# Staging buffers, VectorE instead of GpSimd, and a shorter planner lag in a hybrid decoder step on eight cores

## The chip, the cores and the metric

The kernel runs on the 8 cores of one Trainium2 chip, as two dies of four cores (cores 0 to 3 and 4 to 7). Every core does the same work on its own share of the batch, and no data passes between them. A core has TensorE for matmuls (it writes to PSUM, eight banks in this kernel), VectorE, ScalarE and GpSimd for everything else, and DMA engines, 16 by the profile's pages, that move data between DRAM and the on-chip memory SBUF; in this kernel GpSimd also issues the DMAs that load and cast weights. The metric is device time in microseconds (us) of the slowest core. The experiments ran in four sets on four chips, each set beside runs of the kernel before on the same chip. Some executions here are longer at a lower granted TensorE clock: one of the kernel before took 1599.7 us with cores 0 to 3 at 0.82 to 0.83 and the other four at 0.97, where the median beside it was 1439.01 us.

## The reference, cut to what matters

One decoder layer for a prompt group (one sequence of 2048 rows per core) and a sample group (16 sequences of 4 rows per core) with the same weights:

```python
h = x + W_out( sig(gA) * Wa(GLA(xn)) + sig(gB) * Wb(Pool(xn)) )   # xn = rmsnorm(x)
h = h + CrossAttn(rmsnorm(h), K_mem, V_mem)       # 4 heads, 256 memory tokens
h = h + W_down(relu(W_up rmsnorm(h))**2)
# one projection xn @ w_in gives q, k, v, forget gate, og, u, gA, gB
# GLA output: rmsnorm(o) * silu(og);  Pool: windows 2/4/8/16, mixed, then Wb
```

K_mem and V_mem of the prompt are outputs (`mk`, `mv`). So are the GLA states (`sgp`, `sgs`) and the last pooling rows (`spp`, `sps`).

## The kernel before

The prompt's 2048 rows go through in four tiles of 512 rows. The program first records operations, and a planner then orders them for each engine on a simple cost model. The recorder's helpers own the lines of a profile: L789 is every matmul group of one bank, L801 a group of several, L846 every ScalarE activation, L898 every DMA. So profiles of this kernel are read by tile names.

Each operation carries a priority. Work on the side, that is the one-time precomputation of tile 0 (`pre`) and the sample group's matmuls ("hooks", which use a weight while it is loaded), is recorded with an offset of 120 places. The planner then takes it about that much later than its place in the program says. I call this offset the lag:

```python
    def hook(self, name, *a):              # cut
        self.g.pri_off = po + 120
        self.aux = 1
        f(*a)
    def step(self, name, n=1):             # one piece of a generator: pre, G, K, V, P
        self.g.pri_off = po + 120
        self.aux = 1
        ...  next(g)
    def bank(self):                        # PSUM: 5 banks for the tile, 3 for side work
        lo, n = (5, 3) if self.aux else (0, 5)
```

Weights pass through five slots `wt` of 1 MiB; four more slots, `wx`, lie inside `WqK` and `VWo` and serve until those are written. A weight is cast from fp32 at its first two uses by a GpSimd DMA, stored as bf16 to scratch DRAM at the second (at the first for the up and down weights), and read from there afterwards:

```python
    def W(self, name):                     # cut
        elif times == 0 or (times == 1 and name not in EARLY):
            cast, store = True, times == 1 or name in EARLY
        if cast:  self.dma("pool", flat, src, nb=5.0, ahead=60.0, ...)
        else:     self.dma("sp", flat, self.scr[idx], ...)
        if store: self.dma("sp", self.scr[idx], flat, nb=2.5, ...)
```

A slot can be loaded again only when its matmuls and its store are over. Loads stand in GpSimd's instruction stream in order.

The parts that the change touches, cut: the norm's power, the GLA chunk, the output gate, the branch gates, and in the precomputation the pooled weight b' and `mk`, `mv`:

```python
    def rstd(self, st, P, n=1):
        self.ts("dve", st[:P, :n], st[:P, :n], EPS, ALU.add)
        self.tt("pool", st[:P, :n], st[:P, :n], self.ncols[:P, 8:8 + n], ALU.pow)   # ncols: -0.5
    # tile(): og0, og1 and u0 side by side over the four chunks, then u1
            self.tt("pool", Sb, self.S, pv, ALU.mult)          # decayed state as bf16
            self.act(t, pb, AF.Tanh, scale=0.5)                # og; sig = (1 + tanh)/2
            self.stt("dve", ogb, t, 1.0, pb, ALU.add, ALU.mult)
    # branch gates: ug = W("gb0"), uw = W("bp0"): tanh(pb1), then (t + 1) * pb2 -> t1
    # precompute(): pm @ w_b -> bpt (SBUF); then
            self.dma("sp", self.scr[b], self.bpt[n]); ...      # read back as "bp0", "bp1"
            t = self.tb()                                      # one of four shared tmp
            self.cp("act", t, pb); self.dma("sp", O["mk"], t)
            self.cp("pool", self.Mtm, t)
    # sample: t = self.tb(); cp("act", t, pb); 16 x dma("sp", O["sps"][bb, 11:15], t)
```

## Time and profile before

| | before |
|---|---|
| median of 3 runs | 1434.41 us (1433.49 to 1434.5) |
| best of the 15 runs beside the changed kernel, same chip | 1430.65 us |
| span of core 6 in the profile, granted clock | 1432.6 us, 0.969 |
| TensorE / VectorE / ScalarE / GpSimd busy | 92 / 45 / 36 / 12% |

A busy share of 92% on TensorE with everything else under half says that TensorE sets the time and that the interest lies in its holes. The prediction shows where they are. What it calls cold clock is this: in the 6.4 us after the gap of 14.56 us the granted clock was 0.55 (the last 24 of 32 matmuls of 256 columns took 4.76 us, 0.20 each, where they step by 0.11 in solid stretches), in the 3.6 us after the gap of 6.92 us it was 0.50, and after one of 2.82 us 1.00.

```profile
146.03 0.53 POOL L898 DMA_DIRECT2D wt<-wu  x1 [21.62 <-PE pb L801]
...
161.76 0.53 POOL L898 DMA_DIRECT2D wt<-wu  x1 [15.21 <-PE pb L789]
...
175.57 0.53 POOL L898 DMA_DIRECT2D wt<-wu  x1 [13.29 <-PE pb L789]
```

TensorE is full from 160 to 180 us, so no list of TensorE's gaps shows anything here. But the DMA engines are 60% idle, in a stretch where their share is 0.93 in the 20 us before and 1.01 in the 20 us after. GpSimd asked for only three weights in 30 us, because each load stood 13 to 22 us until matmuls ahead of it were done. The first of them, by the built program the precomputation's weight `xo0`, waits for the last matmuls of `xqT0`, the `KT,wt` group at 143.61 us that the prediction shows: side work of the precomputation, which the lag puts late.

### The profile page before, as it was taken

How to read it: one execution, taken by the hardware profiler on the slowest of the kernel's cores; microseconds unless marked ns; L12 is line 12 of the kernel's file. 1: busy time of each engine (PE TensorE's matmuls, PEld its weight loads, DVE VectorE, ACT ScalarE, POOL GpSimd, SP SyncE). 2: the span in 40 equal slices, each digit the busy share in tenths (PEclk: the TensorE clock that was granted, in tenths of full speed). 3: DMA queues.
4: the chain of work that ended last, by engine and by line, in shares of the span. 5: the costliest groups of instructions: out<-in, count | busy, mean ns of one | idle time of the engine just before them, and what ended most of it. 6: DMA issues, size and time to landing. Idle time of an engine off the chain costs nothing.

```text
span 1432.6 us, 21898 instructions; the slowest of 8 cores (1419.1 to 1432.6 us)
## 1 busy us (share of the span) xinstructions
PE 1311.7 (92%) x7843; PEld 653.7 (46%) x7976; DVE 641.5 (45%) x1114; ACT 512.1 (36%) x1012; POOL 176.4 (12%) x232
## 2 busy tenths in 40 slices
PE   6995979999897979999999899989999999999996
PEld 3452434544343434454444455454454454455443
DVE  3652314643553412454586722464344542354344
ACT  3451214721162411662224631562114451372112
POOL 5121011200111200100010300120011230020000
PEclk7998899999998889999999999999999999999998
DMA  9999698989999998734668333358669895621332
GB/s 205 170 178 193 125 205 161 275 172 219 222 218 241 226 243 201 261 135 148 235 238 276 132 119 118 148 131 228 180 175 214 228 229 192 180 87 59 118 118 96
DMA packets 47094, 261.42 MB, mean 182 GB/s; under 512 B 6054, under 2 KB 6510, under 8 KB 23292
## 3 DMA queue, kind: packets, MB, share of 16 engines
q0 software_dynamic: 15584, 85.38, 36.0%
q1 hardware_dynamic: 31404, 174.63, 34.8%
q8 instruction: 66, 1.08, 0.3%
q14 instruction: 40, 0.33, 0.1%
HBM read 287.63 MB, written 56.36 MB: 240 GB/s over the span
## 4 chain that ended last, share of the span: by engine, by line
PE 68%; DMA 21%; ACT 3%; DVE 3%; issue 3%; POOL 1%; SPq 0%; DVEq 0%; ACTq 0%; POOLq 0%
PE pb L789 62%; DMA wt<-wu 9%; DMA sps<-tmp 3%; PE pb L801 3%; DMA wscratch<-wt 3%; DMA wx<-wscratch 2%; ACT tmp L846 2%; PE pb L822 2%; PE pb L812 2%; DMA mv<-tmp 2%; DMA wt<-wscratch 1%; DMA xh<-xp 1%; DVE stat L884 0%; ACT xn L846 0%; DVE actT L858 0%
## 5 line engine op out<-in xcount | busy, mean ns | idle before, releaser
L789 PE MATMUL pb<-actT,wt 128*128 128x512 bf16 (+2 forms) x1879 | 402.9, 367 | 15.9 <-DMA wt<-wu 4.5
L846 ACT ACTIVATE tmp<-pb 128x512 f32<-128x512 f32 (+1 forms) x250 | 143.6, 587 | 509.1 <-PE pb L789 371.6
L789 PEld LDWEIGHTS pb<-actT,wt 128*128 128x128 bf16 x1920 | 181.2, 98 | 218.9 <-issue 24.4
L789 PE MATMUL pb<-wt,hid 128*128 128x512 bf16 x994 | 227.1, 381 | 8.3 <-DMA wt<-wu 5.4
L789 PE MATMUL pb<-wt,actT 128*128 128x512 bf16 x679 | 162.3, 388 | 10.7 <-DMA wt<-wu 4.3
L789 PEld LDWEIGHTS pb<-wt,hid 128*128 128x128 bf16 x1024 | 97.9, 98 | 126.0 <-issue 15.1
L869 DVE SCALAR_TENSOR_TENSOR xh<-pb,r,xh 128x512 f32<-128x512 f32 x128 | 95.8, 751 | 100.7 <-PE pb L789 100.5
L869 DVE SCALAR_TENSOR_TENSOR hid<-pb,tmp 128x512 bf16<-128x512 f32 x128 | 86.6, 689 | 107.0 <-ACT tmp L846 107.0
L858 POOL TENSOR_TENSOR stat<-stat,ncols 128x1 f32<-128x1 f32 (+3 forms) x71 | 47.4, 669 | 515.4 <-DVE stat L864 513.0
L789 PEld LDWEIGHTS pb<-wt,actT 128*128 128x128 bf16 x704 | 66.7, 99 | 89.3 <-issue 21.9
L846 ACT ACTIVATE xn<-xh 128x512 bf16<-128x512 f32 (+1 forms) x81 | 56.4, 704 | 125.5 <-DVE xh L869 111.1
L898 POOL DMA_DIRECT2D wt<-wu x57 | 31.5, 554 | 405.1 <-PE pb L789 291.7
L789 PE MATMUL pb<-o2T,wt 128*128 128x512 bf16 x251 | 61.1, 387 | 10.2 <-ACT tmp L846 10.0
L869 DVE SCALAR_TENSOR_TENSOR t<-tmp,pb 128x512 f32<-128x512 f32 x32 | 22.0, 687 | 106.2 <-PE pb L789 60.4
L789 PE MATMUL pb<-WqK,actT 128*128 128x512 bf16 x249 | 57.7, 379 | 2.0 <-ACT tmp L846 0.9
L789 PE MATMUL pb<-VWo,PT 128*128 128x512 bf16 x247 | 56.9, 379 | 2.1 <-ACT tmp L846 1.7
L789 PE MATMUL pb<-dT,wt 128*128 128x512 bf16 x223 | 53.3, 383 | 5.9 <-ACT tmp L846 3.4
L789 PE MATMUL pb<-wt,mT 128*128 128x512 bf16 x248 | 56.1, 379 | 2.1 <-DMA wt<-wscratch 1.0
L869 DVE SCALAR_TENSOR_TENSOR tmp<-tmp,pb 128x512 f32<-128x512 f32 (+1 forms) x34 | 22.8, 671 | 63.2 <-PE pb L789 57.5
L822 PE MATMUL pb<-ident,xn 128*128 128x128 bf16 x512 | 40.5, 225 | 9.8 <-DVE xn L864 6.1
L864 DVE TENSOR_SCALAR stat<-stat 128x1 f32<-128x1 f32 (+4 forms) x102 | 20.6, 203 | 58.8 <-ACT xn L846 32.4
L846 ACT ACTIVATE tmp<-pb,stat 128x256 f32<-128x256 f32 (+1 forms) x68 | 37.8, 556 | 23.1 <-DVE stat L884 9.1
(218 smaller groups left out, 1422.7 us busy)
## 6 DMA issues: line engine op xcount, KB each, us to landing
wt<-wscratch SPq DMA_DIRECT2D x87, 1024.0 KB, 5.9
wt<-wu POOLq DMA_DIRECT2D x57, 1024.0 KB, 20.1
wscratch<-wt SPq DMA_DIRECT2D x32, 1024.0 KB, 33.3
land<-xp SPq DMA_DIRECT2D x16, 512.0 KB, 10.3
xh<-xp SPq DMA_DIRECT2D x16, 512.0 KB, 22.0
yp<-xh SPq DMA_DIRECT2D x15, 512.0 KB
s0f<-sgla SPq DMA_DIRECT2D x15, 512.0 KB, 8.3
sgs<-s0f SPq DMA_DIRECT2D x15, 512.0 KB
```

Of the source, the lines that this page charges most:

```text
L789: ins = e.matmul(out, l, r, start=(start and i == 0), stop=(stop and i == m - 1))
L801: ins = e.matmul(out, l, r, start=(i == 0), stop=(i == m - 1))
L812: ins = e.matmul(out, l, r, start=False, stop=last and k == len(al) - 1)
L822: ins = e.transpose(o, i, d)
L846: return self.g.op("act", lambda e: e.activation(out=out, in_=in_, func=func, scale=scale, **kw), reads=rd, writes=wr, cost=c, tab=tab)
L858: return self.g.op(eng, lambda e: e.tensor_tensor(out=out, in0=in0, in1=in1, op=op), reads=[in0, in1], writes=[out], cost=self.vcost(eng, ...
L864: return self.g.op(eng, lambda e: e.tensor_scalar(out=out, in0=in0, scalar1=s1, scalar2=s2, op0=op0, **kw), reads=rd, writes=[out], cost=s ...
L869: return self.g.op(eng, lambda e: e.scalar_tensor_tensor(out=out, in0=in0, scalar=scalar, in1=in1, op0=op0, op1=op1), reads=rd, writes=[ou ...
L898: return self.g.op(q, lambda e: e.dma_start(out=out, in_=in_), reads=[in_], writes=[out], cost=0.6 if q == "pool" else 0.07, dma=True, nb= ...
```

## The change

Its intent is to keep the in-order engines from standing behind one another's waits: ScalarE behind output stores, GpSimd's weight loads behind its arithmetic, weights behind slots that two or three of them hold side by side. Cut to its core (recorder plumbing, sample gates, renamings, and the moves of the softmax product `Pn`, of `pmT` and of the memsets from GpSimd to VectorE left out):

```diff
 # staging buffers; one more tmp
-        self.tmp = [... for i in range(4)]
+        self.tmp = [... for i in range(5)]
+        self.mstage = [g.sb(f"mstage{i}", XH + 8192 + 2048 * i, [128, 512], F32) for i in range(4)]
+        self.ustage = [g.sb(f"ustage{i}", X + o, [64, 512], F32) for i, o in enumerate((7168, 4096))]
-                    t = self.tb()
+                    t = self.ring("mstage", self.mstage)
-                    self.cp("pool", self.Mtm[wh]..., t[:, :])
+                    self.cp("dve", self.Mtm[wh]..., t[:, :])
 # GpSimd keeps only DMA issue; tanh becomes exp, ln, exp
-        self.tt("pool", st, st, self.ncols[:P, 8:8 + n], ALU.pow)
+        self.act(st, st, AF.Ln, bias=EPS);  self.act(st, st, AF.Exp, scale=-0.5)
-                self.tt("pool", Sb, self.S, pv, ALU.mult)
+                self.tt("dve", Sb, self.S, pv, ALU.mult)
-            self.act(t, pb, AF.Tanh, scale=0.5)
+            self.act(t, pb, AF.Exp, scale=-1.0); self.act(t, t, AF.Ln, bias=1.0); self.act(t, t, AF.Exp, scale=-1.0)
 # gates stored at the third use
+STORE_AT.update(dict.fromkeys(("ga0", "ga1", "gb0", "gb1"), 2))
 # b' out of SBUF in tile 0, stored after the attention
-            uw = self.W(f"bp{n}")
+            u = Fixed(self.bpt[n]) if first and br == "b" else self.W(f"{nm}{n}")
 # og0, og1, u0, u1 and the down weights one after another
-        og = [self.W("og0"), self.W("og1")];  u0 = self.W("u0")
+        u = self.W("og0")
+        for s in range(4): ogp(u, 0, s)
+        u = self.W("og1");  ...  u = self.W("u0");  ...  u = self.W("u1")
 # the planner: eight banks placed freely; priorities inherited; the lag
+        for o in reversed(ops):
+            for j in o.succ:
+                o.pri = min(o.pri, ops[j].pri)
     def hook(self, name, *a):
-            self.g.pri_off = po + 120
+            self.g.pri_off = po + 16
     def step(self, name, n=1):
-        self.g.pri_off = po + 120
+        self.g.pri_off = po + (20 if name == "pre" else 120)
```

## The prediction

> **What bounds the kernel now.** I read the table of cores first (spans 1419.1 to 1432.6 us, clocks 0.969 to 0.977, both dies alike: a fast run), then the slices of the page for core 6, the slowest.
>
> ```profile
> PE   6995979999897979999999899989999999999996
> ...
> PEclk7998899999998889999999999999999999999998
> DMA  9999698989999998734668333358669895621332
> ```
>
> Each digit is a slice of 36 us. TensorE is the engine that sets the time (92% busy), but its holes lie in slices 0 to 15, just where the DMA engines are full. From slice 16 on it is nearly solid. So the question is the first 560 us. The forget-gate matmul opens each of the four 512-row tiles, which gives a table of windows by tile:
>
> ```profile
> core 6: us, PE busy (x) PEld busy (x) DVE busy (x) ACT busy (x) POOL busy (x), PEclk, DMA share, GB/s
> 30.50:401.20 370.70, 324.95 (x1746) 160.10 (x1778) 158.75 (x258) 130.01 (x256) 52.94 (x75) 0.96 0.95 193
> 401.20:754.00 352.80, 325.47 (x1781) 154.93 (x1812) 164.62 (x301) 130.76 (x252) 33.53 (x40) 0.96 0.77 215
> 754.00:1091.00 337.00, 321.90 (x2024) 162.92 (x2058) 159.74 (x290) 123.35 (x248) 37.76 (x46) 0.99 0.58 168
> 1091.00:1420.40 329.40, 321.08 (x2139) 163.86 (x2172) 146.69 (x246) 117.99 (x242) 35.21 (x43) 1.00 0.52 154
> ```
>
> What is a tile worth without holes and at full clock? In solid stretches 49 or 50 matmuls of 512 columns take 10.74 us (one record in fifty is missing), 0.215 us each; 256 columns step by 0.11, 128 by 0.056. Counting the built program's matmuls by tile gives 314, 310, 321 and 331 us (estimates; the last is 2 us too high, as that tile took 329). The slack is thus 57, 43, 16 and about 0 us, 116 us in all; before and behind lie 30 us of start (14 of it TensorE work) and 12 us of tail.
>
> Next I listed TensorE's idle stretches and looked at what the engine named there was itself waiting for:
>
> ```profile
> 142.29 0.60 ACT L846 ACTIVATE tmp<-pb 128x512 f32<-128x512 f32 x1 [14.50 <-DMA mk<-tmp]
> ...
> 143.61 1.86 PE L801 MATMUL pb<-KT,wt 128*128 128x256 bf16 x8 [14.56 <-ACT WqK L846]
> ```
> ```profile
> 450.96 0.53 POOL L898 DMA_DIRECT2D wt<-wu  x1 [27.76 <-DMA wscratch<-wt]
> ...
> 458.62 0.37 PE L801 MATMUL pb<-vt,att 128*128 128x256 bf16 x1 [4.75 <-POOL Sb L858]
> ...
> 461.25 1.04 POOL L858 TENSOR_TENSOR stat<-stat,ncols 128x4 f32<-128x4 f32 x1
> ...
> 463.43 0.58 PE L801 MATMUL pb<-vt,kdt 128*128 128x256 bf16 x2 [3.80 <-DVE xn L869]
> ```
> ```profile
> 522.40 1.89 PE L789 MATMUL pb<-o2T,wt 128*128 128x512 bf16 x8 [2.82 <-ACT tmp L846]
> 532.93 3.57 PE L789 MATMUL pb<-o2T,wt 128*128 128x512 bf16 x8 [6.92 <-ACT tmp L846]
> ```
>
> These are two kinds of head-of-line blocking. ScalarE works in order; its next tanh or copy needs one of four shared buffers `tmp`, and that buffer is still being read by an output DMA (mk, mv, sps) which waits in a full DMA system: 14.5 us at 142, 3.4 at 203, 2.8 and 6.9 at 522 and 533. GpSimd also works in order; it issues the weight loads and does arithmetic too, so a load that waits 28 us for a weight slot holds up Sb and the power of the norm (its input was ready at 453, it ran at 461). The rest of the big gaps are weights that came late: 5.4 us at 374, 2.9 at 468, 2.6, 3.5 and 2.4 at 153, 188 and 194 (two of them the pooled weight b', written to DRAM and read back).
>
> [...] the granted clock is 0.84 in the 36 us with the 14.6 us gap, 0.86 in those with the 6.9 us gap and 1.00 in unbroken ones. So a long gap costs more than itself, some 20 us over the first two tiles (each slice's busy time times its missing clock). [...] an 8 KB sps store stood 25 us in the chain. [...] Before has 8 loads of 1283 ns, two a tile, as ln and tanh alternate. [...] Sb on VectorE should cost about 1.2 us, as the 1024-wide norm product does here (actT<-pb,cols, 1218 ns), against 1903 ns on GpSimd.
>
> **The change, part by part.**
> (1) TensorE's work is untouched: 7976 matmuls of the same shapes in both programs.
> (2) mk, mv and sps get staging buffers of their own. Named gain: 14.6 + 3.4 + 2.8 + 6.9 = 27.7 us of idle, plus the cold clock behind it.
> (3) GpSimd keeps only DMA issue; Sb, Pn, casts and pmT go to VectorE, the power of -0.5 to ScalarE as ln and exp. Named gain: 4.75 + 3.8 at 458 to 463, and small waits of that kind in later tiles. VectorE gets 15 x 1.2 of Sb, some 6 of Pn, 5 of casts and pmT, and loses about 70 x 0.2 of adds: +15 us on 641. Harmless.
> (4) In tile 0 b' is used out of SBUF; its two reads go, its stores move behind the attention. Hardware-queue transfers: 174.63 MB in 34.8% of 1432.6 us, 3.0 us per MiB; GpSimd's casting loads: 85.38 MB in 36.0%, 6.3 us per MiB. So tile 0's DMA work falls by 6 us.
> (5) The ga and gb weights are stored at their third use, not the second: four stores, 12 us, leave crowded tile 1; tile 2 pays 4 x (6.3 - 3.0) for loads and 12 for stores, 25 us, where the DMA share is 0.58. Hidden.
> (6) og0, og1, u0, u1 and the down weights are used up one after another instead of two or three side by side, so slots come free sooner and loads are asked for earlier. PSUM: all 8 banks are placed by the planner in place of rings of 5 and 3.
> (7) tanh becomes exp, ln, exp. 96 prompt tiles get two more instructions, 0.69 and 0.60 us from the rows for T and tmp: +124 us. About 71 norms get two small ones at some 0.24 us: +34. Table loads: -9. ScalarE goes from 512 to some 660 us, still half of TensorE. Locally: while the GLA chunks run, ScalarE has 8 x 1.9 + 8 x 0.6 + 16 x 0.57 + 4 x (0.6 + 1.26 + 0.5), about 39 us, against TensorE's 16 x 1.72 + 9, about 37 us. That is level, and new: it was 28.
>
> **The sum.** Tile 0 cannot gain its 57 us: its DMA work is 0.95 x 370.7 = 352 us, after (4) 346, so at most 25 us come out before transfers set the pace; I take 22. Tile 1 holds 352.8 x 0.77 = 272 us of DMA, so only its crowded first half binds. Its named gaps (2.8 + 6.9 + 4.8 + 3.8 + 2.9 = 21 us) and some 10 us of cold clock are removable, a part comes back as a wait for weights: 25. Tile 2: 5 of its 16. Tile 3: nothing. Against it the level ScalarE in the GLA stage, about 1 to 2 us a tile, hidden under transfers in tiles 0 and 1 but not in 2 and 3: -4. Start (first weight lands at 20.6 us, same order of issue) and tail (norm, then the last store) stay. 22 + 25 + 5 - 4 = 48; 1434.4 - 48 is about 1387 us, 3.3% less.
>
> **The rivals.**
> A. The DMA wait takes the place of the wait removed. For it: the DMA digits are 9 nearly throughout slices 0 to 15, and before already waits for weights. Against it: 13 us of DMA idleness at 144 to 180, where the share is 0.63 because TensorE was stuck and no slot came free. If the transfers bind fully, tile 0 gives 11 and tile 1 12 us, and the rest cancels: about 1411.
> B. ScalarE becomes the bound in the GLA stage, banks stay held through three-step sigmoids and TensorE stalls 5 us or more a tile. For it: 39 against 37 us in an in-order engine that also runs the state and sample work. Against it: eight shared banks and a gate stage with room to catch up (16 sigmoids of 1.9 us in the time of 32 matmul groups of 1.72, 30 in 55 us). It takes another 15 us: about 1402.
> C. Everything works and the clock stays up: the slack of tiles 0 and 1 shrinks to 30 us together, tile 2's to 8: about 1355. Against it stands tile 0's DMA floor.
> D. The table set: if the back end put ln and exp in different sets, some 150 switches at 1.3 us would hit the sigmoids: well above 1434. Against it: before's eight loads fit exactly with ln and exp in one set. About 1 in 50.
>
> **Range and chances.** The middle is 1387. A and B together give the upper end, 1412; most of C the lower, 1364. Faster by over 2% means below 1405.7: 0.80. Within 2%: 0.18. Slower: 0.02.
>
> **What would show it.** Right: no TensorE gap with an ACT `tmp` releaser over 2 us in tiles 0 and 1; GpSimd with nothing but DMA issues; one table load; tile windows of about 349, 328, 334 and 331 us; clocks of tiles 0 and 1 up to 0.98; the DMA share of tile 0 at 0.98 or more, its remaining gaps released by weight loads; ACT about 660 us busy, DVE about 655. Wrong: tile 0 near 330 us (its DMA floor was no floor), gaps released by ACT or by DVE products of sigmoids in the GLA stage of tiles 2 and 3 (rival B), or weight waits of 20 us and more in tiles 0 and 1 (rival A).

## More of the kernel before

What ScalarE waited for where that was a DMA (engine, line, tile, releaser: us in total, times, longest):

```profile
ACT tmp L846 <- DMA mk<-tmp: 24.4, 4, 14.5
ACT tmp L846 <- DMA sps<-tmp: 21.7, 2, 11.7
ACT tmp L846 <- DMA mv<-tmp: 20.4, 3, 17.0
...
ACT xn L846 <- DMA land<-xp: 8.0, 4, 4.3
```

ScalarE stood 66.5 us (24.4 + 21.7 + 20.4) behind output stores of a shared buffer. This is what the staging buffers are to remove.

The second is one window of 20 us in tile 0 (length, then busy us and instructions of PE, PEld, DVE, ACT, POOL, then clock, share of the 16 DMA engines, GB/s), and out of the timeline the weight loads that GpSimd issued around it:

```profile
160.00:180.00 20.00, 19.90 (x96) 9.46 (x97) 8.15 (x12) 4.76 (x8) 1.06 (x2) 1.00 0.40 74
```

## The result, and the profile after

| | before | changed |
|---|---|---|
| median, first chip | 1434.41 us | 1406.86 us (12 runs, 1390.43 to 1462.91) |
| ratio of fast runs, first chip | 1 | 0.9771 (95%: 0.9731 to 0.9811) |
| median, second chip | 1439.01 us | 1404.81 us |
| ratio of fast runs, second chip | 1 | 0.9755 (95%: 0.9738 to 0.9771) |

Ratios are the mean time of one kernel's fast runs over that of the other's of the same rounds, so not quite the ratio of the medians. On the first chip the interval straddles the 2% line, so that the verdict there is unclear. The changed kernel's runs fall into groups: five of 1390.4 to 1395.0 us, six of 1406.2 to 1411.8 us in which the slowest core and at least one more have a mean clock of 0.954 to 0.965 (cores elsewhere mostly 0.975 to 0.986; the run of 1395.0 has two such cores too), and the profiled run, 1462.9 us. On the second chip the kernel is faster by over 2%.

The profiled run of the first chip is a slow one, with 0.91 to 0.93 on all eight cores, so its profile explains nothing of the change. Its clock digits and two of its windows are shown once:

```profile
PEclk8998999999998999999999999999888888888887
```
```profile
600.00:1008.00 408.00, 399.95 (x2385) 194.44 (x2426) 213.06 (x380) 189.12 (x382) 6.37 (x12) 0.99 0.59 187
...
1044.00:1400.00 356.00, 349.27 (x1960) 166.78 (x1991) 137.78 (x231) 149.31 (x306) 10.61 (x20) 0.81 0.48 137
```

On this core, 0, the clock is 0.81 from about 1008 us on while TensorE has no gap to speak of (349.27 of 356 us busy), after 400 us at 0.99. No idle time of TensorE comes just before it: from 988 to 1008 us it was busy for 19.89 of 20 us. Nor does the low clock lie on one die: cores 0, 1, 4 and 5 have 0.81 from somewhere between 1000 and 1040 us on, but cores 2, 3, 6 and 7 have 0.80 or 0.81 from the start until about 600 to 640 us, and 0.99 or 1.00 afterwards, with TensorE 97 to 100% busy there in each 20 us from 640 to 700. Each core's times count from its own first instruction, and whether these lie at one moment the profile does not say. What sets this clock was not shown.

All that follows uses the changed kernel's fast profile on the second chip: core 2, 1398.5 us, all cores at 0.974 to 0.981. The helpers' lines have moved: L854, L866, L877 and L887 are the matmuls, L906 ScalarE's activations, L918 to L951 VectorE's operations, L958 the DMAs. First the page's busy times and slices:

```profile
PE 1315.9 (94%) x7976; PEld 652.8 (47%) x7976; DVE 659.1 (47%) x1115; ACT 655.0 (47%) x1359; POOL 60.8 (4%) x117
...
PE   5999899889897899999999989999999989999997
...
PEclk7999999989999899999999999999999999999999
DMA  9999999999999999544586666538399995712331
```

The holes of before in slices 3, 5 and 14 (digits 5, 7 and 7) are gone, and the DMA row is 9 without a break through slice 15. A hole is left in slices 12 and 13 (420 to 490 us; digits 7 and 8). GpSimd went from 176.4 to 60.8 us busy, ScalarE from 512 to 655 us. The windows by tile, cut at the matmul that opens each tile, as in the prediction:

```profile
30.66:384.75 354.09, 326.26 (x1769) 159.99 (x1769) 163.12 (x264) 161.85 (x337) 21.20 (x40) 0.96 1.01 196
384.75:727.86 343.11, 325.27 (x1823) 154.51 (x1822) 167.77 (x300) 166.99 (x339) 8.10 (x15) 0.98 0.79 208
727.86:1058.80 330.94, 322.81 (x2055) 162.97 (x2055) 163.62 (x287) 161.16 (x342) 11.62 (x22) 0.99 0.65 183
1058.80:1386.50 327.70, 320.90 (x2160) 162.78 (x2160) 147.64 (x245) 150.88 (x312) 9.52 (x18) 0.99 0.55 153
```

Single cores differ by some us, so from here on a tile is the median of the eight cores of one profile, cut in the same way. "DMA idle" is the sum over the 28 windows of 20 us up to 560 us of one minus the DMA share (a share above 1 counts as 1), also the median of the cores:

| us | tile 0 | tile 1 | tile 2 | tile 3 and tail | DMA idle to 560 us |
|---|---|---|---|---|---|
| before | 369.0 | 352.3 | 333.3 | 341.3 | 26.7 |
| changed | 348.9 | 340.0 | 330.1 | 339.5 | 4.6 |
| difference | -20 | -12 | -3 | -2 | -22 |

Tile 0 gave what was predicted, tile 1 half of it. What TensorE and ScalarE waited for in the changed kernel:

```profile
PE pb L854 <- DMA wt<-wu: 32.8, 8, 12.5
PE pb L887 <- DVE xn L924: 10.3, 3, 4.5
PE pb L854 <- DVE hid L929: 8.3, 1, 8.3
...
PE pb L854 <- ACT t L906: 1.6, 1, 1.6
```
```profile
ACT xn L906 <- DMA land<-xp: 29.9, 7, 15.4
ACT xns L906 <- DMA xsh<-xs: 18.9, 1, 18.9
ACT s0b L906 <- DMA s0f<-sgla: 14.2, 3, 10.6
```

ScalarE's waits for `mk`, `mv` and `sps` stores are gone, and TensorE's for ScalarE's `tmp` with them. In their place TensorE waits 32.8 us for weights, more than twice the 14.3 us that before waited for the same kind, and ScalarE waits 29.9 us for `land`, the next tile's rows, where it was 8.0. The largest wait of each kind in the timeline:

```profile
433.32 25.82 SPq L958 DMA_DIRECT2D wscratch<-wt  x2
...
441.42 0.54 POOL L958 DMA_DIRECT2D wt<-wu  x1 [22.08 <-DMA wscratch<-wt]
...
447.86 0.54 POOL L958 DMA_DIRECT2D wt<-wu  x1 [5.90 <-DMA wscratch<-wt]
459.00 8.81 PE L854 MATMUL pb<-wt,actT 128*128 128x512 bf16 x32 [12.52 <-DMA wt<-wu]
```
```profile
281.64 1.06 ACT L906 ACTIVATE xn<-land 128x1024 bf16<-128x1024 f32 x1 [15.37 <-DMA land<-xp]
...
283.38 0.69 DVE L929 SCALAR_TENSOR_TENSOR hid<-pb,tmp 128x512 bf16<-128x512 f32 x1 [15.70 <-ACT tmp L906]
...
284.21 6.14 PE L854 MATMUL pb<-actT,wt 128*128 128x512 bf16 x18 [8.26 <-DVE hid L929]
```

The first fence is tile 1's weight `u0`. GpSimd could issue its load, the one at 441, only after 22 us of waiting for a store out of its slot (the built program has `v1` there before it), and 17.6 us later the matmuls began, 12.5 us late. This is the hole in slices 12 and 13. The second fence has the shape that the staging was to abolish: in-order ScalarE behind a DMA (15.4 us), VectorE behind ScalarE, TensorE behind VectorE. Only the transfer is another one.

Costs of moved work, by group (busy us, mean ns, then idle ahead):

```profile
L924 DVE TENSOR_SCALAR Pn<-tmp,stat 128x256 bf16<-128x256 f32 x64 | 18.4, 350 | 1.3
L918 DVE TENSOR_TENSOR Sb<-S,eB 128x1024 bf16<-128x1024 f32 x15 | 18.3, 1218 | 0.5
...
L906 ACT ACT_TABLE_LOAD x1 | 1.3, 1283 | 1.3 <-DVE ncols L941 1.3
```

Sb takes 1218 ns on VectorE as estimated, and there is one table load, of 1283 ns, for all the exp and ln of the kernel. Before has eight: one at 1.34 us, then by turns one before a tile's first tanh (56.92) and one before its ln (408.75), and none between the exp and the ln of tile 0 (33.73 and 36.25).

### The profile page after: what moved, and what is told of

Read it like the earlier page. It is cut to its first block, busy times and chain, and to the rows that moved or that the text cites. A ratio compares the mean times of both kernels' runs of the same rounds, so it can differ in the third digit from the quotient of the medians.

```text
span 1461.3 us, 22400 instructions; the slowest of 8 cores (1435.3 to 1461.3 us)
## 1 busy us (share of the span) xinstructions
PE 1373.9 (94%) x7841; PEld 672.9 (46%) x7976; DVE 659.6 (45%) x1115; ACT 656.6 (45%) x1359; POOL 60.9 (4%) x117
## 4 chain that ended last, share of the span: by engine, by line
PE 69%; DMA 26%; issue 2%; DVE 1%; ACT 1%; SPq 0%; another core or an unknown queue 0%; DVEq 0%; POOL 0%; ACTq 0%; POOLq 0%
PE pb L854 61%; DMA wt<-wu 13%; DMA wscratch<-wt 7%; PE pb L866 3%; DMA land<-xp 3%; PE pb L887 2%; PE pb L877 2%; DMA va<-cv 1%; DMA wt<-wscratch 1%; DMA s0f<-sgla 1%; ACT tmp L906 1%; SPq L958 0%; DVE actT L918 0%; DVE xh L929 0%; DVE xn L929 0%
## 5 line engine op out<-in xcount | busy, mean ns | idle before, releaser
L854 PE MATMUL pb<-actT,wt 128*128 128x512 bf16 (+2 forms) x1874 | 422.9, 380 | 21.7 <-DMA wt<-wu 11.1
L854 PEld LDWEIGHTS pb<-actT,wt 128*128 128x128 bf16 x1920 | 186.0, 101 | 238.6 <-issue 92.7
L854 PE MATMUL pb<-wt,hid 128*128 128x512 bf16 x997 | 244.9, 403 | 9.8 <-DMA wt<-wu 5.8
L906 ACT ACTIVATE tmp<-pb 128x512 f32<-128x512 f32 (+1 forms) x172 | 98.3, 586 | 262.2 <-PE pb L854 217.7
L854 PE MATMUL pb<-wt,actT 128*128 128x512 bf16 x677 | 166.8, 399 | 20.9 <-DMA wt<-wu 16.7
L854 PEld LDWEIGHTS pb<-wt,hid 128*128 128x128 bf16 x1024 | 101.4, 102 | 140.7 <-issue 71.7
L906 ACT ACTIVATE xn<-xh 128x512 bf16<-128x512 f32 (+1 forms) x81 | 56.1, 702 | 143.1 <-DVE xh L929 97.8
L918 DVE TENSOR_TENSOR t<-t,pb 128x512 f32<-128x512 f32 x64 | 44.0, 688 | 166.7 <-ACT t L906 142.0
L854 PEld LDWEIGHTS pb<-wt,actT 128*128 128x128 bf16 x704 | 69.2, 101 | 104.9 <-issue 52.3
L906 ACT ACTIVATE t<-pb 128x512 f32<-128x512 f32 x64 | 38.1, 596 | 107.7 <-PE pb L854 107.6
L918 DVE TENSOR_TENSOR xh<-pb,xh 128x512 f32<-128x512 f32 x64 | 42.7, 688 | 63.9 <-PE pb L854 63.3
L958 POOL DMA_DIRECT2D wt<-wu x60 | 32.0, 534 | 896.0 <-PE pb L854 318.0
L854 PE MATMUL pb<-wt,mT 128*128 128x512 bf16 x250 | 62.3, 407 | 3.2 <-DMA wt<-wu 2.9
L854 PE MATMUL pb<-o2T,wt 128*128 128x512 bf16 x252 | 62.5, 393 | 0.3
L854 PE MATMUL pb<-VWo,PT 128*128 128x512 bf16 x249 | 60.4, 393 | 0.4
L854 PE MATMUL pb<-WqK,actT 128*128 128x512 bf16 x247 | 59.7, 393 | 0.6 <-issue 0.2
L854 PE MATMUL pb<-dT,wt 128*128 128x512 bf16 x188 | 48.0, 398 | 3.5 <-DMA wt<-wscratch 3.2
L887 PE MATMUL pb<-ident,xn 128*128 128x128 bf16 x512 | 41.2, 228 | 10.6 <-DVE xn L924 9.9
L906 ACT ACTIVATE t<-t,ncols 128x512 f32<-128x512 f32 x64 | 46.2, 722 | 5.5
L906 ACT ACTIVATE tmp<-pb,stat 128x256 f32<-128x256 f32 (+1 forms) x68 | 37.9, 557 | 20.8 <-DVE stat L924 11.9
```

The costliest lines, as they stand in the source:

```text
L854: ins = e.matmul(out, l, r, start=(start and i == 0), stop=(stop and i == m - 1))
L887: ins = e.transpose(o, i, d)
L906: return self.g.op("act", lambda e: e.activation(out=out, in_=in_, func=func, scale=scale, **kw), reads=rd, writes=wr, cost=c)
L918: return self.g.op(eng, lambda e: e.tensor_tensor(out=out, in0=in0, in1=in1, op=op), reads=[in0, in1], writes=[out], cost=self.vcost(eng, ...
L958: return self.g.op(q, lambda e: e.dma_start(out=out, in_=in_), reads=[in_], writes=[out], cost=0.6 if q == "pool" else 0.07, dma=True, nb= ...
```

## The experiments

The prediction's theory is that the gain is the removal of named head-of-line waits, above all by the staging buffers and by an empty GpSimd. Its rivals are that the transfers of the first two tiles are the floor, so that only what takes work or idle time from the DMA engines counts, and that the order of work (lag, banks, weight order) is what counts. Every edit also lets the planner order all instructions anew, so a run measures an edit together with the new order. Every kernel here gave a correct result. Ratios are to the kernel before, with the 95% interval.

**The changed kernel again**, no edit.

> The changed kernel once more, to have a profile in the fast state. Theory (the transfers pace tiles 0 and 1 once the in-order blocking is gone): undisturbed cores at 1370 to 1391 us, ratio 0.97 to 0.98; no TensorE gap over 1 us released by ScalarE's tmp, one table load, the gaps left in tiles 0 and 1 released by weight loads, some 25 to 35 us of them, the largest near 450 us and about 13 us long. Rival (ScalarE binds in the GLA stage): gaps released by ScalarE or by VectorE's gate products in tiles 2 and 3.

Measured: 0.9755 (0.9738 to 0.9771). This is the kernel that its variants below are held against. A step of 0.001 is 1.4 us. The expectation came true: in the profile above the weight waits of tiles 0 and 1 sum to 27.5 us, the largest ends at 459 us and is 12.5 us long, and no wait of TensorE for `tmp` is left.

**The kernel before with the staging buffers.** The sample's state generator then has to start after the O projection, as in the changed kernel, since it would overwrite `ustage`.

```diff
+        self.mstage = [...]; self.ustage = [...]
-                    t = self.tb()
+                    t = self.ring("mstage", self.mstage)
-                t = self.tb();  self.cp("act", t[:64, :], self.pb[b][:64, :])
+                t = self.ustage[n];  self.cp("act", t[:, :], self.pb[b][:64, :])
-                    self.gen["G"] = self.states()
+            def o_(uo):
+                self.gen["G"] = self.states()
```

> The kernel before with staging buffers of their own for mk, mv and sps (and the state generator started after the output projection, which the shared memory needs), nothing else. Theory: the four ScalarE gaps (27.7 us) go, but in tile 0 weight loads take their place, so 10 to 18 us come out: ratio 0.988 to 0.993. If the named gaps were worth their length plus cold clock, 30 us or more: 0.979 or less. If staging is worth nothing because transfers bind: 0.998 or more.

Measured: 1.0053 (1.0038 to 1.0067), slower, where a gain was expected. ScalarE no longer waits for `mk`, `mv` or `sps` anywhere, so the edit did what it was meant to do. But TensorE's waits for weights became 38.8 us in 12 places, against 14.3 in 6:

```profile
PE pb L791 <- DMA wt<-wu: 38.8, 12, 11.7
PE pb L791 <- DMA wt<-wscratch: 11.1, 5, 8.4
```
```profile
250.19 7.04 PE L791 MATMUL pb<-wt,mT 128*128 128x512 bf16 x24 [11.75 <-DMA wt<-wu]
```

A wait of 14.6 us was taken away, and one of 11.75 us came 100 us later at the O projection, among others. DMA idle rose from 26.7 to 35.7 us. The prediction's theory fails for its largest part: the named gaps went, and the time did not.

**The changed kernel with Sb and the norm's power on GpSimd.**

```diff
-        self.act(st, st, AF.Ln, bias=self.ncols[:P, 6:7]);  self.act(st, st, AF.Exp, scale=-0.5)
+        self.ts("dve", st, st, EPS, ALU.add);  self.tt("pool", st, st, self.ncols[:P, 8:8 + n], ALU.pow)
-                self.tt("dve", Sb[:, :, :], self.S[:, :, :], pv..., ALU.mult)
+                self.tt("pool", Sb[:, :, :], self.S[:, :, :], pv..., ALU.mult)
```

> The changed kernel with Sb and the norm's power back on GpSimd, between the DMA issues. Theory: in tile 1 GpSimd still stands 20 us at a time waiting for a weight slot, so TensorE waits for Sb or xn again, but mostly in the shadow of the late weight: 3 to 10 us slower than the changed kernel, ratio to before 0.979 to 0.984. If GpSimd's blocking was the main cause: 15 us or more slower, 0.988 or above. If it was only in the shadow: no difference.

Measured: 0.9826 (0.9812 to 0.984), 10 us slower than the changed kernel (0.0071 x 1439). Tiles 0 and 1 together take 689.4 us against 688.9, tiles 2 and 3 take 4.0 and 4.2 us more. (Only the sum of the first two can be compared. This planner put a group of 32 matmuls of tile 0 behind the matmul that opens tile 1, so that the tiles by themselves read 337.7 and 351.7.) So an empty GpSimd is worth something, but not where the prediction had put most of it. In tile 1 the changed kernel's wait of 12.5 us for a weight is not in this profile. In its place TensorE waits 4.83 and 5.04 us for GpSimd's arithmetic (Sb, then the power), which stands behind weight loads, the first of them that of the same weight, `u0` by the built program:

```profile
445.00 0.60 POOL L958 DMA_DIRECT2D wt<-wu  x1 [21.27 <-DMA wscratch<-wt]
...
461.81 1.66 DVE L929 SCALAR_TENSOR_TENSOR xn<-pb,stat,ogs 128x256 bf16<-128x256 f32 x4 [7.37 <-POOL stat L918]
...
462.83 6.06 PE L854 MATMUL pb<-wt,actT 128*128 128x512 bf16 x16 [5.04 <-DVE xn L929]
```

So the gap that the prediction named at 458 to 463 us and the late weight lie in each other's shadow: to take one away brings the other out, and no time.

**The changed kernel with the gates stored at their second use.**

```diff
-STORE_AT.update(dict.fromkeys(("ga0", "ga1", "gb0", "gb1"), 2))
```

> The changed kernel with the ga and gb weights stored at their second use, in tile 1, as before. Theory (tile 1's first half is paced by transfers and by slots held until their store is done): 4 stores of 3 us and the waits behind them come back, 8 to 15 us slower than the changed kernel, ratio 0.982 to 0.988. Rival (the DMA is not the bound there): within 3 us of the changed kernel.

Measured: 0.9771 (0.9757 to 0.9786), 2 us slower with intervals that overlap. By the time this is the outcome that the rival had named (within 3 us), not the theory's. By tiles it does what a floor of transfers would do: tiles 0 and 1 take 700.5 us in place of 688.9, so the four stores cost 11 to 12 us there, and tile 2 gets 5.1 of them back (325.0 against 330.1). The tiles are of one profiled run each, and these two are 7.6 us apart (1407.73 and 1400.08), more than the runs as a whole.

**The changed kernel with b' written and read back in tile 0.**

```diff
-                u = Fixed(self.bpt[n]) if first and br == "b" else self.W(f"{nm}{n}")
+                u = self.W(f"{nm}{n}")
+            self.dma("sp", self.scr[UNITS[f"b{n}"][0]], self.bpt[n]..., nb=2.5, wtok=[...])   # in precompute
```

> The changed kernel with the pooled weight b' written to DRAM and read back in tile 0, as before. First theory (6 us of DMA work back in a full tile 0): 5 to 8 us slower than the changed kernel. Second theory, from the first runs (what counts is that a weight slot is free early enough for the DMA engines never to idle; two more loads hold two slots and the read waits for its own store): the DMA share of tile 0 falls below 1.0 and 8 to 15 us are lost. If only GpSimd's and ScalarE's blocking counted: no difference.

Measured: 0.9823 (0.98 to 0.9846), 10 us slower, all of it in tile 0 (359.6 against 348.9). The DMA share of tile 0 is 0.99 on every core, where it was 1.01 or 1.02, as the second theory had it.

**The changed kernel with the down weights in pairs.**

```diff
-            if c < 3:            # one weight after another
+            if False:            # ud = [W(dn_0), W(dn_1)] side by side for every c
```

> The changed kernel with the two halves of a down weight used side by side again. Slot theory: two slots are held for 13.8 us each instead of one for 6.9, so loads of the next tile are asked for later; the DMA engines have idle time in the MLP of tile 0 and tile 1's weights come later: 5 to 12 us slower than the changed kernel. If only the count of bytes matters: no difference, under 2 us.

Measured: 0.9758 (0.9738 to 0.9778), no difference. The expectation was missed: this order of weights does not matter.

**The changed kernel with og0, og1 and u0 side by side**, as before.

```diff
-        u = self.W("og0")
-        for s in range(4): ogp(u, 0, s)      # then og1, u0, u1 in turn between the chunks
+        og = [self.W("og0"), self.W("og1")];  u0 = self.W("u0")
+            ogp(og[0], 0, c);  ogp(og[1], 1, c);  ...  uproj(u0, 0, c)     # in every chunk
```

> The changed kernel with og0, og1 and u0 used side by side over the four GLA chunks and u1 after them, as before. Slot theory: three of the slots are held over some 40 us, so in tiles 0 and 1 the DMA share falls and weight waits grow: 8 to 20 us slower than the changed kernel. If only bytes matter: under 2 us, or a gain, since ScalarE's sigmoids lie further apart.

Measured: 0.9715 (0.9693 to 0.9737), if anything faster than the changed kernel, against the expectation. The late weight is still there: TensorE has stood 16.54 us when it goes on at 454.72. So that wait is not due to the order of og and u.

**The changed kernel without staging buffers.**

```diff
-                    t = self.ring("mstage", self.mstage)
+                    t = self.tb()
-                t = self.ustage[n]
+                t = self.tb()
```

> The changed kernel with mk, mv and sps written out of the shared tmp ring again. If staging is worth something once the slots no longer bind: ScalarE stands behind full DMA queues again, gaps of 5 to 15 us released by tmp near 115, 155 and 480 us, 10 to 25 us slower than the changed kernel. If staging only moves the wait to the weights, as alone on the kernel before: under 3 us.

Measured: 0.9734 (0.9708 to 0.976). The staging is worth nothing in the finished kernel. In its profile ScalarE waits for no store of `tmp` at all; this is every wait of ScalarE for a DMA:

```profile
ACT xns L906 <- DMA xsh<-xs: 27.4, 1, 27.4
ACT xn L906 <- DMA land<-xp: 14.7, 6, 4.3
ACT s0b L906 <- DMA s0f<-sgla: 3.9, 2, 3.2
```

So something else in the change had taken those waits away; which part, no run shows (there are five buffers `tmp` now, for one).

**The changed kernel with 5 and 3 banks.** The planner places again, but in two groups as before and with no spare bank required.

```diff
-            n = sum(1 for k in open_b if banks[k][0] <= t)
-            return n >= len(need) + spare
+            part = PART[self.bclass[need[0]]]           # PART = ({0..4}, {5..7})
+            n = sum(1 for k in open_b if k in part and banks[k][0] <= t)
+            return n >= len(need)
```

> The changed kernel with PSUM split again, 5 banks for the prompt and 3 for the sample and precompute work, still placed by the planner. What the runs so far leave open: of the 35 us, GpSimd's arithmetic holds 10 and b' out of SBUF 10; staging, the down order and the og order hold nothing. If the banks hold the rest: 8 to 15 us slower than the changed kernel. If the transfers of the first 560 us are all that counts (the DMA engines idle 30 us of them in the kernel before, 3 to 9 in the changed one): under 4 us.

Measured: 0.9723 (0.9706 to 0.9739). The free placing of eight banks brings nothing.

**The changed kernel with the lag of before.**

```diff
     def hook:  -  self.g.pri_off = po + 16
                +  self.g.pri_off = po + 120
     def step:  -  self.g.pri_off = po + (20 if name == "pre" else 120)
                +  self.g.pri_off = po + 120
```

> The changed kernel with the planner's lag for precompute, sample hooks and steps set back to 120 places everywhere (now 20 for precompute, 16 for hooks). DMA theory: the precompute of tile 0 then runs late and keeps its weight slots long, the DMA engines idle 10 us or more in the first 560 us and 8 to 15 us are lost. If the lag does not matter: under 3 us.

Measured: 1.0102 (1.0081 to 1.0122), 1453.92 us against 1440.01 of before. Undoing the two constants costs 50 us ((1.0102 - 0.9755) x 1440), more than the whole gain and over three times what was expected. Tiles 0, 1 and 2 take 371.5, 350.3 and 347.8 us; DMA idle is 26.5 us. What happened in tile 0, in windows of 20 us:

```profile
180.00:200.00 20.00, 20.00 (x107) 9.54 (x105) 7.48 (x12) 8.94 (x15) 1.06 (x2) 1.00 0.62 119
200.00:220.00 20.00, 9.85 (x46) 4.25 (x44) 6.92 (x11) 5.00 (x9) 1.59 (x3) 0.84 1.00 178
220.00:240.00 20.00, 8.09 (x24) 2.98 (x24) 3.14 (x5) 1.64 (x3) 0.00 (x0) 0.67 0.79 161
240.00:260.00 20.00, 19.10 (x109) 9.77 (x110) 7.53 (x19) 17.33 (x43) 2.67 (x5) 0.89 0.62 150
```
The DMA engines fall to 0.62 while TensorE is full (180 to 200 us), and TensorE pays 20 to 40 us afterwards (9.85 and 8.09 of 20 us busy): 11.97 us of waiting for an O projection weight. Why it was late shows in the order of GpSimd's loads in the two built programs, and in when they were issued:

```
changed:   ...  ga1  a1  o0  o1   up0  up1  up2  up3
long lag:  ...  ga1  a1  o1  up1  up2  o0   dn0_0  up0
```
```profile
174.92 0.53 POOL L958 DMA_DIRECT2D wt<-wu  x1 [6.38 <-PE pb L866]
193.96 0.53 POOL L958 DMA_DIRECT2D wt<-wu  x1 [18.51 <-PE pb L854]
195.69 0.53 POOL L958 DMA_DIRECT2D wt<-wu  x1 [1.20 <-PE pb L887]
...
203.48 0.53 POOL L958 DMA_DIRECT2D wt<-wu  x1 [7.27 <-PE pb L854]
...
221.82 3.57 PE L854 MATMUL pb<-wt,mT 128*128 128x512 bf16 x8 [11.97 <-DMA wt<-wu]
```

With the long lag these are `o1`, `up1`, `up2` and, at 203.48, `o0`. In the changed kernel `o0` goes out at 175.63, and the same window has no such hole:

```profile
175.63 0.53 POOL L958 DMA_DIRECT2D wt<-wu  x1 [7.26 <-PE pb L854]
```
```profile
180.00:200.00 20.00, 20.00 (x95) 9.03 (x93) 7.99 (x14) 12.92 (x21) 1.06 (x2) 1.00 1.00 178
```

In both programs `o0` has the slot of `xo0`, the last but one weight of the precomputation. The long lag puts `xo0`'s matmuls late, so the planner loads two weights of the MLP first, which nobody needs yet, and the weight that TensorE needs next comes 28 us later. In tile 2 the hooks do the same: a load there stood 55.35 us behind sample matmuls, and a matmul group of the tile then waited 10.56 us (883.93 and 898.23 us in the profile).

**The kernel before with b' out of SBUF in tile 0.**

```diff
-            uw = self.W(f"bp{n}")
+            uw = Fixed(self.bpt[n]) if first else self.W(f"bp{n}")
     # stores of bpt moved from precompute to behind the attention
```

> The kernel before with b' used out of SBUF in tile 0 and its stores put behind the attention, nothing else. DMA theory: the idle time of the DMA engines in the first 560 us falls from 30 to some 15 us, and 8 to 14 us come out of the time: ratio 0.990 to 0.994. If, as with staging alone, one part alone only moves the wait: 0.997 to 1.006.

Measured: 1.0066 (1.0046 to 1.0086), slower, though it takes DMA work away, so the DMA theory's expectation failed; nearest is the other one, that one part alone only moves the wait. DMA idle rose from 26.7 to 38.1 us: with the lag of 120 the planner's new order has the same hole, 160 to 180 us at a DMA share of 0.39, and more behind it.

**The kernel before with the short lag only.**

```diff
     def hook:  -  self.g.pri_off = po + 120
                +  self.g.pri_off = po + 16
     def step:  -  self.g.pri_off = po + 120
                +  self.g.pri_off = po + (20 if name == "pre" else 120)
```

> The kernel before with only the planner's lag changed: 20 places for precompute and 16 for the sample's hooks in place of 120. Undoing the lag in the changed kernel cost 50 us, more than the whole gain. If the lag carries the gain by itself: ratio 0.970 to 0.985, the second xqT weight used by 140 us instead of 177, DMA idle time in the first 560 us down from 30 to under 12 us. If it needs the other parts (with ScalarE still standing behind mk and mv and GpSimd behind the loads, earlier precompute runs into those waits sooner): 0.990 to 1.005, with ScalarE's tmp gaps still there.

Measured: 0.9948 (0.9909 to 0.9987), 7 us by the ratio, 10 by the medians (1421.83 against 1432.28); the ratio takes in a run of 1438.4 us with one die at 0.957 to 0.967. Tile 0 gains 11 us (358.1), tile 1 nothing (353.9). The hole at 160 to 180 us is closed without any staging (share 1.02). The gap of 14.6 us in the `xqT0` matmuls is gone; the next weight's, `KT,wx`, begin at 133.84 after 1.03 us, and the load of `xo0` goes out at 133.36 in place of 146.03:

```profile
160.00:180.00 20.00, 13.19 (x59) 5.54 (x58) 2.82 (x5) 2.98 (x5) 4.04 (x7) 0.88 1.02 203
```
```profile
133.84 3.73 PE L801 MATMUL pb<-KT,wx 128*128 128x256 bf16 x28 [1.03 <-ACT WqK L846]
```
```profile
PE pb L789 <- DMA wt<-wu: 17.3, 6, 6.0
PE pb L789 <- ACT tmp L846: 15.1, 7, 7.2
```

TensorE's waits for ScalarE's `tmp` (15.1 us) are as long as before (16.0), though, the largest still in tile 1, at 512 and 522 us. The short lag alone is not the change.

**What the runs have in common.** In twelve of thirteen kernels tile 0 plus tile 1 is 685 us, plus the DMA idle time, plus 12 us where the four gate stores lie in tile 1; 685 is fitted, 12 is the prediction's estimate for the stores. A part of the rows:

| us | tiles 0 + 1 | DMA idle | stores | 685 + idle + stores |
|---|---|---|---|---|
| before | 721 | 26.7 | 12 | 724 |
| before, staging | 735 | 35.7 | 12 | 733 |
| before, b' | 732 | 38.1 | 12 | 735 |
| before, lag | 712 | 13.3 | 12 | 710 |
| changed | 689 | 4.6 | 0 | 690 |
| changed, gates early | 700 | 4.7 | 12 | 702 |
| changed, b' reloaded | 699 | 12.5 | 0 | 698 |
| changed, long lag | 722 | 26.5 | 0 | 712 |

The twelve fit within 5 us; the last row is the one that does not, by 10. As a rule found after the fact it is an observation. What supports it is that it puts kernels in order that have very different lists of TensorE gaps.

The side-by-side, the 5 and 3 banks and the unstaged version beat both kernels in their runs (0.9715, 0.9723 and 0.9734 against 0.9755), by 0.2 to 0.4%, with intervals that touch or overlap and on other chips. Their combination was not run.

## Why the prediction was right or wrong

The time was right: 1387 us with a range of 1364 to 1412, against a median of 1406.86 (its faster group 1390 to 1395) and 1404.81 on a second chip. So was the class, faster by over 2%, on the second chip clearly, while the first leaves it unclear. The gain was 28 to 34 us in place of 48. That it lies within the range is in part luck: the largest named part, staging, was worth nothing, and the lag, which the prediction does not mention, was needed.

*The bound.* Right. TensorE's holes in the first 560 us were nearly the whole matter: tiles 0 and 1 gave 32 of the 37 us. Transfers do fill tile 0 now (share 1.01 or 1.02 on every core), as the prediction's floor says. But that the measured 349 comes so near to its 346 is partly luck. The bytes moved in tile 0 fell, from 71.6 to 68.9 MB (rate times length, median of the cores), while the busy time of the DMA engines, share times length, stayed at some 352 us and did not fall by 6.

*Tile 0, -22.* Measured -20, so the size is right, but by luck, for it came from other parts than were named. Staging: 0 (348.3 without it). The short lag brings 11 us by itself, and undoing the b' part costs 10.7 us in the finished kernel. The prediction had 6 us of DMA work for b', and never mentioned the lag, although both changed lines stand in the diff: it had only asked which instruction each part adds or removes, and the lag adds and removes none.

*Tile 1, -25.* This term was mis-sized: measured -12. The step that failed is "Its named gaps (2.8 + 6.9 + 4.8 + 3.8 + 2.9 = 21 us) and some 10 us of cold clock are removable, a part comes back as a wait for weights: 25". The gaps went and core 2's clock in this tile is 0.98 where core 6 had 0.96 before, but a 12.5 us wait for the `u` weight came; it stands near 445 to 468 us in six of the variants' profiles too (11.6 to 16.5 us; with the long lag 10 to 11 us, at 474 to 479 us, read on four cores), whatever the staging, the banks or the weight order. In the traces it follows from a line that the prediction itself quotes: the load at 450.96 that waited 27.76 us for a store out of its slot. By the built program this is the same weight, `u0`, behind the same store, `v1`. The prediction read this as a nuisance for the arithmetic behind it in GpSimd. The load was what was left: with Sb and the power put back it waits 21.27 us for its slot in place of 22.08, the arithmetic's waits take the place of the weight's, and tiles 0 and 1 change by 0.5 us. No run took that store away, so its part is read from the traces, not tested.

*Gates at the third use, "hidden".* Mechanism right, place in the sum wrong: the stores were left out of tile 1's sum, and by tiles they are most of its gain (10 of 12 us; tile 1 is 350.1 with early stores, 340.0 without). Tile 2 pays 5.1 us, so it is not quite hidden.

*Tiles 2 and 3.* Predicted -5 in tile 2 and +4 for a level ScalarE; measured -3 and -2. The feared level ScalarE cost nothing to be seen: 655 us busy as estimated (660), one TensorE wait of 1.6 us behind a sigmoid. GpSimd's relief, listed for tile 1 with no more than small waits in later tiles, works here, 8.2 us.

*Rivals.* A (DMA waits take the place) is half true: 32.8 us of weight waits instead of 14.3, tile 1 at its 12 us, tile 0 not at its 11. The sign that the prediction had set for it, weight waits of 20 us and more in tiles 0 and 1, came true (27.5 of the 32.8 us lie there), next to most of the signs of being right. B and D are refuted by the 1.6 us and by the single table load. C did not happen: tiles 0 and 1 kept 65 us (689 less 314 and 310) in place of its 30. The upper end of the range covers A alone, 1411; with the 15 us of B it would be 1426.

*Weight order and banks, part 6.* The prediction gave them no number of their own, and taking back the down weights, og and u, or the banks cost nothing.

*What stays open.* The parts undone in the finished kernel add up to over 70 us, twice the gain, so they are not shares of it. Single parts put into the kernel before make it slower by 0.5 and 0.7%; the profiles show the DMA idle time that goes with it, not why the planner's new orders have it. The lag is worth 50 us as undone and 7 to 10 us alone, so it works together with other parts; which, was not isolated. The lag of the hooks and that of the precomputation were not run apart: tile 0 has no hooks, so its share is the precomputation's, and tile 2 has no precomputation, so the 18 us there with the long lag are put down to the hooks, as long as no effect of tile 0 reaches that far. Priority inheritance, the fifth `tmp`, the sigmoid as exp, ln, exp, and the other moves to VectorE were not tested by themselves. Neither was what triggers the clock of 0.96 on some cores; the runs with single cores at 0.954 to 0.965 beside cores of the same die at 0.98 have no profile.

## What to carry to other kernels

Where weights stream through a few slots and the DMA engines are near full, look for windows in which the DMA engines are idle although TensorE is busy (before: a share of 0.40 from 160 to 180 us, TensorE busy for 19.90 of 20): in these kernels that idle time came back later as a gap with another name (with the long lag, a share of 0.62 from 180 to 200 us and a wait of 11.97 us for a weight at 221.82). What closed it was to free slots earlier (the short lag alone: 1.02 in the window from 160 to 180), while removing the named gap alone made the kernel slower (1.0053). So a gap's releaser need not be what limits: with the staging left out of the finished kernel it took 0.9734, against 0.9755 with it. Ask of each load not only who waits for it but what it waits for: `u0`'s stood 22.08 us behind a store out of its slot, where a store of 1 MiB is 3.0 us of the engines' time by the prediction's estimate. And read a scheduler's constants in a diff as closely as its instructions: here undoing two offsets cost five times what undoing any rewritten part did.
